# Gate row of a modulation in 1024-wide sums, and two sets of rounded projection weights in place of three

## The chip, the cores and the metric

The kernel runs on one core of a Trainium2 chip. The metric is the device time of one execution in microseconds (us). The kernel before was timed in three runs: median 555.95 us, from 555.89 to 556.93. Its profile is of one further execution, which took 556.66 us, of which the profiled span is 554.9 us.

The engines are named as in the profile: PE is TensorE (matmul), PEld its weight load, DVE is VectorE, ACT is ScalarE, POOL is GpSimd, SP is SyncE, whose queue issues all DMAs here. An engine executes its instructions in the order of its own list. A line number such as L542 is a line of the kernel before.

## What is computed

One decoder layer for 1024 tokens of width 1024, in fp32, cut to what matters here:

```
(shift, scale, gate) = silu(c) @ w_mod + b_mod        # w_mod: 1024 x 3072
h    = rmsnorm(x) * g_pre * (1 + scale) + shift
proj = h @ w_in                                       # the columns go to three head groups
y    = concat(mLSTM, sliding-window attention, stick-breaking attention)   # each gated by silu(z)
x    = x + gate * rmsnorm(y @ w_out) * g_post
```

The gate is one row of 1024 numbers: for column j the sum over the 1024 inputs d of silu(c)[d] * w_mod[d, 2048 + j], plus a bias.

## The kernel before

**Precision.** A weight matrix is used as two rounded parts: the hi part is a cast on ACT (L300), the lo part is the difference on POOL (L302, in two halves of 512 columns). A projection is three products: hi by hi, lo by hi, hi by lo.

**Projection items.** PE works through a list of items. Two are token-major (`mif`, `av`, class ProjT, L385). Sixteen are column blocks of `w_in` (class ProjD, L359), each with 48 matmuls of 128x512: 24 for the first 512 tokens, 24 for the second. The order at the start is mif, ak (block d7), av, then aq0, aq1, aq2 (d4, d5, d6), then the blocks of the stick-breaking heads and of the gates z. From aq1 on, the items are cut into pieces of a few matmuls, which stand between the matmuls of the head groups (`fill(n)`).

**Weights of an item.** `prep_load` issues the DMA of a block (512 KB) into a staging tile `w_d`, of which there are two. `prep_split` makes `wh_d` and `wl_d`; of these there are `nw` sets, three in this kernel. A set can be written again when PE has done the item that used it. Both steps have a raised priority.

**Order.** PE's order is written out by hand. That of DVE, ACT, POOL and SP is by hand up to the first projection; from there on a scheduler lays them out by readiness and priority.

**Start of the stretch.** While PE runs `mif`, DVE makes a causal convolution of three blocks of 128x1024: three products (L506) and nine sums (L509), in the order tap 1 of the blocks 0, 1, 2, then tap 2, then tap 3. Each finished block goes through a sigmoid on ACT (`cusg`, L513, two buffers) and a product on POOL (`cu`, L514). ACT's copies that empty the PSUM banks of `mif` (L446, L447) stand behind these sigmoids in ACT's list. PE's projections alternate between two banks.

**Gate row.** While PE runs `av`, the gate row is summed on DVE (`gate_row`, L534 to L542): column block by column block of 256, each in 8 products of 128x256 with one number of silu(c) per partition, added up in `gacc`. So there are 4 TENSOR_SCALAR and 28 SCALAR_TENSOR_TENSOR. The weights come in eight DMAs of 512 KB (`wg`, four buffers). On PE, behind the last matmul of `av`, `gate_sum` adds up the 128 partitions by a product with ones (`gbps`, L551), once for each half of 512 columns; DVE adds the bias (L552) and POOL multiplies (L553). Then aq0 runs through.

**What follows.** Behind aq0 the mLSTM chunks start. Of chunk c, `qps` (L674) and `kps` (L684) come first, then `sps` (L693), `cps` (L699) and `nps` (L715). `nps` needs `am` (L695 on DVE), the product of `sps` with a decay matrix `e`. That matrix comes from DVE (L664, when the DMA `mbc` has landed), then POOL's mask (L665), then ACT's exponential (L667).

Of the kernel before, what the change touches and what calls it, by code (L numbers as in the profile page):

```python
# [10 lines left out]
F32 = mybir.dt.float32  # L11
F32R = mybir.dt.float32r
AF = mybir.ActivationFunctionType
ALU = mybir.AluOpType
# [3 lines left out]
P = 128  # L18
D = 1024
S = 1024  # L20
KT = 8
# [25 lines left out]
def trunk(ctx: ExitStack, tc, x, w_ss, w_gate, rows, cols, w_mu, w_mif, w_dm, w_av, wqk, bif, alibi, w_out,  # L47
          out):
    nc = tc.nc
    V, A, G, T = nc.vector, nc.scalar, nc.gpsimd, nc.tensor  # L50

    def pool(name, bufs=1, side="left", space=None, stack=ctx):
        kw = dict(name=name, bufs=bufs, reuse_waits="tile")
        if space is not None:
            kw["space"] = space
        else:
            kw["side"] = side
        return stack.enter_context(tc.tile_pool(**kw))

    def f32(ap):  # L60
        return ap.bitcast(F32) if ap.dtype == F32R else ap

    def load(dst, src):
        nc.sync.dma_start(f32(dst), f32(src))
# [26 lines left out]
    csil = cp.tile([P, KT], F32, name="csil")  # L91
# [189 lines left out]
    tw = pool("tw", side="right", stack=tw_stk)  # L281
# [3 lines left out]

    def prep_load(key, src, shape, tok=False):
        n = int(np.prod(shape))
        p, w, nw = (tw, "t", 4) if tok else (fw, "w", 3)
        size = 2 * MIF if tok else D
        z = p.tile([P, size], F32, tag=w + "32", bufs=2, name=f"w_{key}")  # L290
        with tc.high_priority(offset=0 if tok else WPRI):
            load(z[:, 0:n], src)
        wready[key] = (z, n, shape, p, w, nw, size)
# [11 lines left out]
    def prep(key, src, shape, tok=False):  # L305
        prep_load(key, src, shape, tok)
        prep_split(key, tok)
# [26 lines left out]
    fw = pool("fw", stack=fw_stk)  # L334
    stg = pool("stg", stack=fw_stk)

    class ProjD:
# [5 lines left out]
        def prep(self, stage):  # L343
            if self.halves[0] == 0:
                if stage == 0:
                    prep_load(f"d{self.ti}", w_dm[self.ti], (KT, P))
                else:
                    prep_split(f"d{self.ti}")
# [156 lines left out]
    for j in range(3):  # L505
        V.tensor_scalar(out=cu[:, j, :], in0=mup[:, j, 0:S], scalar1=col[:, C_CW + 4 * j:C_CW + 4 * j + 1],  # L506
                        scalar2=col[:, C_CB + j:C_CB + j + 1], op0=ALU.mult, op1=ALU.add)
        for tap in range(1, 4):
            V.scalar_tensor_tensor(out=cu[:, j, :], in0=mup[:, j, tap:tap + S],  # L509
                                   scalar=col[:, C_CW + 4 * j + tap:C_CW + 4 * j + tap + 1], in1=cu[:, j, :],  # L510
                                   op0=ALU.mult, op1=ALU.add)
# [16 lines left out]
    def gate_row():  # L528
        gacc = gp_.tile([P, D], F32, name="gacc")
        rowb = gp_.tile([P, 2, D], F32, name="rowb")  # L530
        load(rowb, rows.partition_broadcast(P))
        for s_ in range(4):
            a = gacc[:, s_ * 256:(s_ + 1) * 256]
            for q in range(2):  # L534
                w = gw.tile([P, 4, 256], F32, tag="wg", bufs=4, name=f"wg{s_}_{q}")
                load(w, w_gate[s_][:, 4 * q:4 * q + 4, :])
                for i in range(4):
                    c = csil[:, 4 * q + i:4 * q + i + 1]
                    if q + i == 0:
                        V.tensor_scalar(out=a, in0=w[:, 0, :], scalar1=c, scalar2=None, op0=ALU.mult)  # L540
                    else:
                        V.scalar_tensor_tensor(out=a, in0=w[:, i, :], scalar=c, in1=a, op0=ALU.mult, op1=ALU.add)  # L542
        return gacc, rowb

    def gate_sum():
# [45 lines left out]
    for h in range(MH):  # L591
        V.tensor_tensor_scan(out=mp[:, 4 + h:36:4], data0=ga[:, h:32:4], data1=ga[:, 32 + h:64:4], initial=0.0,
                             op0=ALU.max, op1=ALU.add)
# [30 lines left out]
    gw_stk = ExitStack()  # L624
    gw = pool("gw", stack=gw_stk)
    gacc, rowb = gate_row()
    fill(GF[3])
    fill.through(I_AQ)
# [520 lines left out]
def lay_out(inputs):  # L1149
    f = {k: np.asarray(v) for k, v in inputs.items()}  # L1150
    w_mod = f["w_mod"][0]
    wm = w_mod.reshape(KT, P, 3, D)
    w_ss = wm[:, :, 0:2, :].reshape(KT, P, 2, KT, P).transpose(3, 1, 0, 2, 4).reshape(KT, P, KT, 2 * P)
    w_gate = wm[:, :, 2, :].reshape(KT, P, 4, 256).transpose(2, 1, 0, 3)
    b_mod = f["b_mod"][0].reshape(3, D)
    colT = lambda v: v.reshape(-1, P).T
    cw = f["m_conv_w"][0].reshape(4, 3, P).transpose(2, 1, 0).reshape(P, 12)
    cols = np.concatenate([colT(b_mod[0]), colT(b_mod[1]), colT(f["g_pre"][0]), colT(f["c"][0]), cw,
                           colT(f["m_conv_b"][0]), colT(f["m_norm_g"][0]), colT(f["m_skip"][0]),
                           np.broadcast_to(f["a_sinks"][0], (P, AH))], axis=1)  # L1160
    rows = np.stack([b_mod[2], f["g_post"][0]])
    w = f["w_in"][0]
    w_mu = w[:, 0:384].reshape(KT, P, 384)
    tok = lambda m: m.reshape(4, 2, P, m.shape[1]).transpose(0, 2, 1, 3).reshape(4, P, 2 * m.shape[1])
    w_mif = tok(w[:, 384:776])
    w_av = tok(np.concatenate([w[:, 1672:1800], w[:, 2696:2952]], axis=1))
    dm = [w[:, o + j * P:o + (j + 1) * P].reshape(KT, P, P).transpose(1, 0, 2).reshape(P, D)
          for o, n in ((2184, 2), (2440, 2), (1160, 3), (1544, 1), (776, 3), (1800, 3), (2952, 2)) for j in range(n)]
    wqk = np.stack([f["m_wq"][0].transpose(2, 0, 1), f["m_wk"][0].transpose(2, 0, 1)], axis=1)
    bif = np.stack([np.tile(f["m_b_i"][0], NT), np.tile(f["m_b_f"][0], NT)], axis=1)  # L1170
    slopes = (2.0 ** (-8.0 * np.arange(1, AH + 1) / AH)).astype(np.float32)
    rel = P + np.arange(P)[:, None] - np.arange(2 * P)[None, :]
    ok = (rel >= 0) & (rel < P)
    alibi = np.where(ok[None], -slopes[:, None, None] * rel.astype(np.float32), np.float32(NEG))
    return dict(x=f["x"][0], w_ss=w_ss, w_gate=w_gate, rows=rows, cols=cols, w_mu=w_mu, w_mif=w_mif,
                w_dm=np.stack(dm), w_av=w_av, wqk=wqk, bif=bif, alibi=alibi.astype(np.float32).transpose(1, 0, 2),
                w_out=f["w_out"][0].reshape(KT, P, D))
# [17 lines left out]
```

## Time and profile before

| | us |
|---|---|
| median of three runs | 555.95 |
| the profiled execution | 556.66 |
| its span | 554.9 |
| PE busy | 527.5 (95%) |
| DVE busy | 336.3 (61%) |
| ACT busy | 250.5 (45%) |
| POOL busy | 222.4 (40%) |
| DMA, mean rate over the span | 174 GB/s |

The busy share of PE counts its time at either clock level: the table of 40 slices shows a granted clock below full speed in two places besides the first and last slices, at about 83 to 97 us and 152 to 166 us. The chain that ended last runs over PE for 80% of the span, over DVE for 10%, over ACT for 5%. A wait of another engine counts for the end only where PE waits for it in turn.

### The profile page before, as it was taken

The page shows a single profiled execution, that of the slowest core. Times are in us where ns is not written, and L with a number is a line of the kernel's source. Part 1 is how long each engine was busy: PE and PEld are TensorE (multiplying, and loading weights), DVE is VectorE, ACT ScalarE, POOL GpSimd, SP SyncE. Part 2 cuts the span into 40 slices and gives each one's busy share as a digit, 9 for nine tenths or more (in the row PEclk, how much of TensorE's full clock was granted, in tenths as well). Part 3 has the DMA queues.
Part 4 walks back from the last instruction along what each step waited for, and adds up shares of the span by engine and source line. Part 5 has one row for each costly group of instructions (what it writes and reads, how often), then busy time and mean ns, then how long its engine had stood idle before and what let it go on. Part 6 is the DMA issues. An engine that isn't in the chain of part 4 may idle for free.

```text
span 554.9 us, 8574 instructions
## 1 busy us (share of the span) xinstructions
PE 527.5 (95%) x2953; PEld 452.3 (82%) x2953; DVE 336.3 (61%) x774; ACT 250.5 (45%) x571; POOL 222.4 (40%) x206
## 2 busy tenths in 40 slices
PE   4799997999979999999999999999999999999995
PEld 3577897989958998877788788888888888788884
DVE  5686692053835778669797669787887443108232
ACT  5643442351103333336877668676767332114100
POOL 2355796340014253324343456683765333111000
PEclk9999997999989999999999999999999999999998
DMA  8981451127976455399964269555211159606421
GB/s 298 418 310 57 139 206 59 57 98 188 322 219 210 149 172 153 104 265 259 251 205 138 92 186 281 170 129 194 96 59 76 39 171 403 245 16 236 144 80 71
DMA packets 63659, 96.57 MB, mean 174 GB/s; under 512 B 17600, under 2 KB 36992, under 8 KB 63488
## 3 DMA queue, kind: packets, MB, share of 16 engines
q1 hardware_dynamic: 63616, 96.03, 54.5%
q8 instruction: 23, 0.38, 0.3%
q14 instruction: 20, 0.16, 0.1%
HBM read 69.24 MB, written 25.20 MB: 170 GB/s over the span
## 4 chain that ended last, share of the span: by engine, by line
PE 80%; DVE 10%; ACT 5%; issue 2%; POOL 1%; DMA 1%; DVEq 0%; POOLq 0%; SPq 0%; ACTq 0%
PE pd L359 26%; PE ptav L385 6%; PE mu L233 6%; PE op L1112 5%; PE op L1111 5%; PE op L1110 5%; PE ptmif L385 3%; PE tp L997 3%; DVE cu L509 3%; ACT zb L850 3%; PE ops L1016 2%; PE ops L1015 2%; DVE zb L860 2%; PE z L966 2%; PE xps L166 2%
## 5 line engine op out<-in xcount | busy, mean ns | idle before, releaser
L359 PE MATMUL pd<-hh,wh_d 128*128 128x512 f32 x256 | 72.2, 407 | 0.0
L359 PE MATMUL pd<-hh,wl_d 128*128 128x512 f32 x256 | 71.2, 400 | 0.0
L359 PE MATMUL pd<-hl,wh_d 128*128 128x512 f32 x256 | 70.6, 398 | 0.0
L359 PEld LDWEIGHTS pd<-hh,wh_d 128*128 128x128 f32 x256 | 47.1, 192 | 8.9 <-issue 0.6
L359 PEld LDWEIGHTS pd<-hl,wh_d 128*128 128x128 f32 x256 | 46.1, 188 | 8.1
L359 PEld LDWEIGHTS pd<-hh,wl_d 128*128 128x128 f32 x256 | 45.9, 189 | 7.8
L302 POOL TENSOR_TENSOR wl_d<-w_d,wh_d 128x512 fp32r<-128x512 f32 x32 | 46.5, 1475 | 13.5 <-ACT wh_d L300 13.5
L1112 PE MATMUL op<-wol,hh 128*128 128x512 f32 x128 | 50.7, 396 | 0.0
L1110 PE MATMUL op<-woh,hh 128*128 128x512 f32 x128 | 50.6, 396 | 0.0
L1111 PE MATMUL op<-woh,hl 128*128 128x512 f32 x128 | 50.6, 396 | 0.0
L71 DVE TENSOR_TENSOR al<-tp,ah 128x512 fp32r<-128x512 f32 (+2 forms) x56 | 27.4, 494 | 19.9 <-ACT ah L70 19.6
L985 POOL TENSOR_TENSOR sg<-sg,pr 128x512 f32<-128x512 f32 (+1 forms) x30 | 31.1, 1041 | 19.7 <-DVE pr L983 19.4
L860 POOL TENSOR_SCALAR zb<-zb,mx 128x256 f32<-128x256 f32 (+1 forms) x24 | 21.6, 911 | 41.9 <-ACT ph L70 17.0
L70 ACT CAST ah<-tp 128x512 fp32r<-128x512 f32 (+2 forms) x56 | 24.4, 437 | 28.7 <-PE tp L997 21.5
L1123 ACT ACTIVATE sj<-op 128x512 f32<-128x512 f32 x16 | 9.5, 597 | 50.2 <-PE op L1112 47.7
L1112 PEld LDWEIGHTS op<-wol,hh 128*128 128x128 f32 x128 | 24.0, 188 | 6.0 <-POOL wol L71 0.2
L1111 PEld LDWEIGHTS op<-woh,hl 128*128 128x128 f32 x128 | 24.0, 188 | 5.9
L1110 PEld LDWEIGHTS op<-woh,hh 128*128 128x128 f32 x128 | 24.0, 188 | 5.8
L1127 POOL TENSOR_TENSOR st<-st,mhalf 128x1 f32<-128x1 f32 x8 | 4.4, 555 | 57.2 <-DVE st L1126 57.2
L850 ACT ACTIVATE zb<-zb,mx 128x256 f32<-128x256 f32 (+1 forms) x48 | 23.2, 485 | 8.3 <-DVE mx L840 6.7
L983 DVE TENSOR_TENSOR_SCAN pr<-z,mzero 128x128 f32<-128x128 f32 (+3 forms) x32 | 25.5, 813 | 1.0 <-ACT z L974 0.7
L385 PE MATMUL ptmif<-wh_mif,hh 128*128 128x392 f32 x64 | 23.2, 362 | 3.0 <-ACT igf L447 3.0
(247 smaller groups left out, 1338.7 us busy)
## 6 DMA issues: line engine op xcount, KB each, us to landing
wm<-in_w_ss_dram SPq DMA_DIRECT2D x16, 512.0 KB, 7.9
w_d<-in_w_dm_dram SPq DMA_DIRECT2D x16, 512.0 KB, 3.8
xt<-in_x_dram SPq DMA_DIRECT2D x8, 512.0 KB, 8.3
wg<-in_w_gate_dram SPq DMA_DIRECT2D x8, 512.0 KB, 6.3
wo<-in_w_out_dram SPq DMA_DIRECT2D x8, 512.0 KB, 5.4
xr<-in_x_dram SPq DMA_DIRECT2D x8, 512.0 KB, 4.4
out_dram<-ot SPq DMA_DIRECT2D x16, 256.0 KB, 2.4
hh<-d_yh SPq DMA_DIRECT2D x12, 256.0 KB, 5.8
```

What stands on the lines that cost most here:

```text
L71: e_lo.tensor_tensor(out=dst_l, in0=src, in1=dst_h.bitcast(F32), op=ALU.subtract)
L233: T.matmul(mu_acc[j][n], w[:, cs], h[:, k, t], start=(k == 0 and w is wh and h is hh), stop=(k == KT - 1 and h is hl))
L302: G.tensor_tensor(out=wl[:, a:b], in0=z[:, a:b], in1=wh.bitcast(F32)[:, a:b], op=ALU.subtract)
L359: T.matmul(ps, w[:, k, :], h[:, k, t], start=(k == 0 and w is wh and h is hh), stop=(k == KT - 1 and h is hl))
L385: T.matmul(ps[:, 0:self.N], h[:, k, t], w[:, k % 2, :], start=(k == 0 and q == 0), stop=(k == KT - 1 and q == 2))
L850: A.activation(z, z, AF.Exp, bias=nm[:, h:h + 1], accum_out=sm[:, h:h + 1])
L860: (G if h >= 6 - NPOOL else V).tensor_scalar(out=z, in0=z, scalar1=sm[:, h:h + 1], scalar2=None, op0=ALU.mult)
L983: V.tensor_tensor_scan(out=rev(pr), data0=rev(zps), data1=mzero[:, 0:1].to_broadcast([P, w]), initial=1.0 if nxt is None else nxt, op0=ALU ...
L985: (G if w > 256 and (h > 0 or i > 3) else V).tensor_tensor(out=sg[:, 0:w], in0=sg[:, 0:w], in1=pr[:, 1:w + 1], op=ALU.mult)
L1110: T.matmul(o, hh[:, k, t], woh[:, k, cs], start=(k == 0), stop=False)
L1111: T.matmul(o, hl[:, k, t], woh[:, k, cs], start=False, stop=False)
L1112: T.matmul(o, hh[:, k, t], wol[:, k, cs], start=False, stop=(k == KT - 1))
```

## The change

The gate weights are laid out by blocks of 128 inputs instead of blocks of 256 columns, and the gate row is summed in eight instructions of 128x1024 (one TENSOR_SCALAR, seven SCALAR_TENSOR_TENSOR). The DMAs are still eight of 512 KB, with 4 KB per partition in one piece. The sets of `wh_d` and `wl_d` are two instead of three.

```diff
     def prep_load(key, src, shape, tok=False):
         n = int(np.prod(shape))
-        p, w, nw = (tw, "t", 4) if tok else (fw, "w", 3)
+        p, w, nw = (tw, "t", 4) if tok else (fw, "w", 2)
...
-        for s_ in range(4):
-            a = gacc[:, s_ * 256:(s_ + 1) * 256]
-            for q in range(2):
-                w = gw.tile([P, 4, 256], F32, tag="wg", bufs=4, name=f"wg{s_}_{q}")
-                load(w, w_gate[s_][:, 4 * q:4 * q + 4, :])
-                for i in range(4):
-                    c = csil[:, 4 * q + i:4 * q + i + 1]
-                    if q + i == 0:
-                        V.tensor_scalar(out=a, in0=w[:, 0, :], scalar1=c, scalar2=None, op0=ALU.mult)
-                    else:
-                        V.scalar_tensor_tensor(out=a, in0=w[:, i, :], scalar=c, in1=a, op0=ALU.mult, op1=ALU.add)
+        for k in range(KT):
+            w = gw.tile([P, D], F32, tag="wg", bufs=4, name=f"wg{k}")
+            load(w, w_gate[k])
+            c = csil[:, k:k + 1]
+            if k == 0:
+                V.tensor_scalar(out=gacc, in0=w, scalar1=c, scalar2=None, op0=ALU.mult)
+            else:
+                V.scalar_tensor_tensor(out=gacc, in0=w, scalar=c, in1=gacc, op0=ALU.mult, op1=ALU.add)
...
-    w_gate = wm[:, :, 2, :].reshape(KT, P, 4, 256).transpose(2, 1, 0, 3)
+    w_gate = wm[:, :, 2, :]
```

The scheduler lays out the lists of DVE, ACT, POOL and SP anew; PE's list stays as it is, but for line numbers. Lines from L543 on have a number lower by three in the changed kernel.

DVE, from the third last piece of `av` to the end of the gate row (`vsl5` to `vsl7` empty the banks of `av`; `wg3_1` is the second half of the inputs of the last column block). Before:

```order
L71 TENSOR_TENSOR vsl6_1497<-ptav_6_1471,vsh6_1496 128x384
L542 SCALAR_TENSOR_TENSOR gacc_1328<-wg2_1_1361,csil_73,gacc_1328 128x256 x2
L540 TENSOR_SCALAR gacc_1328<-wg3_0_1367,csil_73 128x256
L542 SCALAR_TENSOR_TENSOR gacc_1328<-wg3_0_1367,csil_73,gacc_1328 128x256 x3
L542 SCALAR_TENSOR_TENSOR gacc_1328<-wg3_1_1373,csil_73,gacc_1328 128x256
L552 TENSOR_TENSOR gbc_74<-gbps0_1534,rowb_1329 128x512
L542 SCALAR_TENSOR_TENSOR gacc_1328<-wg3_1_1373,csil_73,gacc_1328 128x256
L71 TENSOR_TENSOR vsl7_1528<-ptav_7_1502,vsh7_1527 128x384
L542 SCALAR_TENSOR_TENSOR gacc_1328<-wg3_1_1373,csil_73,gacc_1328 128x256 x2
L552 TENSOR_TENSOR gbc_74<-gbps1_1538,rowb_1329 128x512
```

The same place in the changed kernel:

```order
L71 TENSOR_TENSOR vsl5_1442<-ptav_5_1416,vsh5_1441 128x384
L539 SCALAR_TENSOR_TENSOR gacc_1328<-wg5_1346,csil_73,gacc_1328 128x1024
L539 SCALAR_TENSOR_TENSOR gacc_1328<-wg6_1349,csil_73,gacc_1328 128x1024
L71 TENSOR_TENSOR vsl6_1473<-ptav_6_1447,vsh6_1472 128x384
L539 SCALAR_TENSOR_TENSOR gacc_1328<-wg7_1352,csil_73,gacc_1328 128x1024
L71 TENSOR_TENSOR vsl7_1504<-ptav_7_1478,vsh7_1503 128x384
L549 TENSOR_TENSOR gbc_74<-gbps0_1510,rowb_1329 128x512
L549 TENSOR_TENSOR gbc_74<-gbps1_1514,rowb_1329 128x512
```

Before, the bias addition of the first half (L552, it waits for PE) stands ahead of the last three sums and of `vsl7`. Now all sums stand ahead of `vsl7` and of both bias additions.

POOL, from the last weights of `av` to the second chunk of the mLSTM (`d7`, `d4`, `d5`, `d6`, `d0` are the blocks of ak, aq0, aq1, aq2 and the first stick-breaking item; `e0`, `e1` the decay matrices of the chunks 0 and 1; the rows of L746 prepare the output of a chunk). Before:

```order
L302 TENSOR_TENSOR wl_d6_1713<-w_d6_1664,wh_d6_1712 128x512 x2
L553 TENSOR_TENSOR gbc_74<-gbc_74,rowb_1329 128x512 x2
L665 AFFINE_SELECT e0_1566<-e0_1566 128x512
L665 AFFINE_SELECT e1_1658<-e1_1658 128x512
L746 TENSOR_TENSOR cu_799<-cu_799,col_62 128x3x128
L302 TENSOR_TENSOR wl_d0_2040<-w_d0_1967,wh_d0_2039 128x512 x2
L746 TENSOR_TENSOR cu_799<-cu_799,col_62 128x3x128
```

The same place in the changed kernel:

```order
L302 TENSOR_TENSOR wl_d5_1563<-w_d5_1548,wh_d5_1562 128x512 x2
L550 TENSOR_TENSOR gbc_74<-gbc_74,rowb_1329 128x512 x2
L302 TENSOR_TENSOR wl_d6_1689<-w_d6_1640,wh_d6_1688 128x512 x2
L743 TENSOR_TENSOR cu_799<-cu_799,col_62 128x3x128
L662 AFFINE_SELECT e0_1542<-e0_1542 128x512
L662 AFFINE_SELECT e1_1634<-e1_1634 128x512
L743 TENSOR_TENSOR cu_799<-cu_799,col_62 128x3x128
```

Further up in POOL's list the split of d5, third behind d7 and d4 and ahead of the three products L514, has gone; every block is now split one item later. Here the split of the next block and the product of L746 have moved ahead of the masks of `e0` and `e1`.

ACT at the same place (`sh_aq0_1` empties the bank of the second half of aq0). Before:

```order
L421 ACTIVATE sh_aq0_0_1604<-pd4_0_1574 128x512
L667 ACTIVATE e0_1566<-e0_1566 128x512
L667 ACTIVATE e1_1658<-e1_1658 128x512
L421 ACTIVATE sh_aq0_1_1635<-pd4_1_1610 128x512
L300 CAST wh_d0_2039<-w_d0_1967 128x1024
L677 COPY q1_0_1646<-qps0_1641 96x512
```

The same place in the changed kernel:

```order
L421 ACTIVATE sh_aq0_0_1580<-pd4_0_1550 128x512
L300 CAST wh_d6_1688<-w_d6_1640 128x1024
L421 ACTIVATE sh_aq0_1_1611<-pd4_1_1586 128x512
L674 COPY q1_0_1622<-qps0_1617 96x512
L664 ACTIVATE e0_1542<-e0_1542 128x512
L664 ACTIVATE e1_1634<-e1_1634 128x512
```

The cast has moved ahead of the evacuation of the same item's second half, here and at the ends of nearly all later items, and the exponentials of `e0` and `e1` behind the copy of `q`.

## Rows read from the trace of the kernel before

**Rows 1.** PE's waits over the span: total us, times, longest us.
```profile
PE gbps L551 <- DVE gacc L542: 3.2, 1, 3.2
PE ptmif L385 <- ACT igf L447: 3.0, 1, 3.0
```
**Rows 2.** Windows: us; PE, PEld, DVE, ACT, POOL busy (count); PEclk; DMA share; GB/s.
```profile
90.80:94.00 3.20, 3.14 (x10) 3.14 (x11) 0.09 (x1) 0.46 (x3) 3.13 (x2) 0.50 0.00 0
...
260.00:270.00 10.00, 9.10 (x54) 7.83 (x53) 8.31 (x32) 7.36 (x24) 3.32 (x4) 1.00 1.08 257
```
**Rows 3.** Timeline of PE around the first wait: start us, us, instruction [idle before].
```profile
87.54 0.33 PE L385 MATMUL ptmif<-wl_mif,hh 128*128 128x392 f32 x1
90.86 0.70 PE L385 MATMUL ptmif<-wh_mif,hh 128*128 128x392 f32 x1 [2.98 <-ACT igf L447]
...
96.90 0.34 PE L385 MATMUL ptmif<-wh_mif,hh 128*128 128x392 f32 x1
```
**Rows 4.** Timeline of ACT, the third sigmoid of the convolution.
```profile
89.32 1.06 ACT L513 ACTIVATE cusg<-cu 128x1024 f32<-128x1024 f32 x1 [2.36 <-POOL cu L514]
```
**Rows 5.** Timeline of POOL, splits beside the convolution.
```profile
70.62 12.96 POOL L302 TENSOR_TENSOR wl_d<-w_d,wh_d 128x512 fp32r<-128x512 f32 x6 [3.40 <-ACT wh_d L300]
```
**Rows 6.** Timeline of DVE: all nine sums of the convolution, then its last two.
```profile
69.98 17.08 DVE L509 SCALAR_TENSOR_TENSOR cu<-mup,col,cu 128x1024 f32<-128x1024 f32 x9
...
84.59 2.47 DVE L509 SCALAR_TENSOR_TENSOR cu<-mup,col,cu 128x1024 f32<-128x1024 f32 x2
```
**Rows 7.** Timeline of PE, from the gate row to the first chunk.
```profile
153.31 1.02 PE L551 MATMUL gbps<-gacc,ones 128*128 128x512 f32 x2
157.52 1.26 PE L551 MATMUL gbps<-gacc,ones 128*128 128x512 f32 x2 [3.19 <-DVE gacc L542]
158.05 3.99 PE L359 MATMUL pd<-hh,wh_d 128*128 128x512 f32 x8
161.87 2.00 PE L359 MATMUL pd<-hh,wl_d 128*128 128x512 f32 x8
...
170.96 1.04 PE L674 MATMUL qps<-cuh,gm 96*96 96x128 f32 x8
...
176.15 1.03 PE L715 MATMUL nps<-v,am 128*128 128x97 f32 x8
```
**Rows 8.** Timeline of DVE in the gate row.
```profile
134.42 1.53 DVE L542 SCALAR_TENSOR_TENSOR gacc<-wg,csil,gacc 128x256 f32<-128x256 f32 x3
...
140.11 1.53 DVE L542 SCALAR_TENSOR_TENSOR gacc<-wg,csil,gacc 128x256 f32<-128x256 f32 x3 [2.34 <-DMA wg<-in_w_gate_dram]
...
154.36 0.69 DVE L552 TENSOR_TENSOR gbc<-gbps,rowb 128x512 f32<-128x512 f32 x1 [0.73 <-PE gbps L551]
...
155.83 1.54 DVE L542 SCALAR_TENSOR_TENSOR gacc<-wg,csil,gacc 128x256 f32<-128x256 f32 x2
```
**Rows 9.** The tile wg: SP's issue ns (min/median/max), first and last start; landing.
```profile
L64 SPq DMA_DIRECT2D wg<-in_w_gate_dram x8: 384/746/1863, 129.5 to 146.3; - x8
...
DMA to landing us min/median/max: 4.5/6.3/7.0
```
**Rows 10.** The chain of waits, the shortest stretch of a whole item.
```profile
448.10 10.89 PE pd L359 x48
```
**Rows 11.** Timeline of POOL at the first chunk.
```profile
167.77 1.56 POOL L665 TENSOR_SCALAR_AFFINE_SELECT e<-e 128x512 f32<-128x512 f32 x2 [6.92 <-DVE e L664]
172.41 0.83 POOL L746 TENSOR_TENSOR cu<-cu,col 128x384 f32<-128x384 f32 x1 [3.08 <-PE kps L684]
173.20 2.50 POOL L302 TENSOR_TENSOR wl_d<-w_d,wh_d 128x512 fp32r<-128x512 f32 x2
```
**Rows 12.** Timeline of ACT at the first chunk.
```profile
168.78 1.22 ACT L667 ACTIVATE e<-e 128x512 f32<-128x512 f32 x2 [2.46 <-POOL e L665]
...
171.70 1.04 ACT L300 CAST wh_d<-w_d 128x1024 fp32r<-128x1024 f32 x1
```
**Rows 13.** Timeline of DVE at the first chunk.
```profile
166.96 1.28 DVE L664 TENSOR_TENSOR e<-tcol,mbc 128x512 f32<-128x512 f32 x2
```

## The prediction

> **What bounds the kernel now.** I read the table of PE's waits first. PE works almost throughout, so the end moves by what PE waits, and by the clock at which it runs. Behind the start, the two longest waits are one of 3.2 us for the gate row's sum, and one of 3.0 us for ACT's copy of the gate pre-activations [rows 1]. The change touches both places.
>
> Next I looked at what each wait leaves behind. Where the first one ends, PE is granted 0.50 of its clock, which is the lower of its two levels, 1.2 GHz [rows 2]. The timeline shows the price: from the start at 90.86 to the start at 96.90 there are 18 steps in 6.04 us [rows 3]. A step of 512 columns takes 10.89 / 48 = 0.227 us at full clock [rows 10], so 392 columns should take 0.174 (an estimate by the columns), and 18 steps 3.1 us. The low clock costs 2.9 us, about as much as the wait itself. The second wait does the same: eight matmuls take 3.99 us behind it and eight later ones 2.00 [rows 7].
>
> Then I followed each wait back. The first: the copy stands in ACT's list behind the third sigmoid, which waits for a buffer that POOL's first product frees at 89.3 [rows 4]; that product waits for the first block's sigmoid, and this one for the seventh sum on DVE, which ends where the eighth starts, at 84.59 [rows 6]. The second: the gate row's last sums run at 155.8, though PE ended `av` at 153.3, because in DVE's list a bias addition that waits for PE's first product stands ahead of them and runs at 154.36 [rows 7, 8].
>
> **First place: one split less beside the convolution.** Sums beside POOL's splits take long: the first seven need 84.59 - 69.98 = 14.6 us, the last two, alone, 2.47 together, so 1.24 each [rows 6]. The first of the seven ran mostly alone, which leaves (14.6 - 1.2) / 6 = 2.23 for each of the six beside POOL's six halves, which took 12.96 / 6 = 2.16 each [rows 5]. The two engines work in turns: 2.23 is 1.24 of DVE and 1.0 of POOL. Without the split of d5 POOL does four halves, and the sixth and seventh sum run alone: 2 x 0.99 = 2.0 us. All behind it comes 2.0 earlier: the first sigmoid, POOL's product, the third sigmoid, the copy, PE. (At 83.7 the ninth sum and POOL's first product now want to start together. Whichever goes first, the third sigmoid needs the end of both, so the chain is as long.) The next matmul could have started at 87.54 + 0.17 = 87.71. It starts at 90.86, and will at 88.9: 1.2 us stay.
>
> Does 1.2 us still lower the clock? A stretch with 0.9 us of idle time ran at full clock [rows 2]. That is the nearest row, so I take no fall and a gain of 2.0 + 2.9 = 4.9 us. With the fall it is 2.0.
>
> **Second place: the gate row.** Now 28 sums at 1.53 / 3 = 0.51 us and four products become eight instructions of 1024 columns. The same operation and width alone took 1.24, beside POOL 2.23, and four narrow ones take 2.04 [rows 6, 8]; I take 1.24, since POOL has no splits to do there. The first load stays where it is; the second landed at 140.1 [rows 8]. From there: sums 1 and 2 to 142.6, `vsl4`, sums 3 and 4 to 145.6. A buffer is free at its first use now, not after four sums, so the last load's issue, 146.3 before [rows 9], follows the third sum at about 144.5. With the median of 6.3 us it lands at 150.8 and with the longest of 7.0 at 151.5 [rows 9]; the last sum ends at 152.1 to 152.8, ahead of 153.3. No bias addition stands in front of it any more.
>
> So PE goes on at 153.3. The two products need 2 x 1.02 us at most, aq0 starts at 155.3 and takes 10.9, and the first chunk begins at 166.2 in place of 170.96 [rows 7, 10]. The gain is 4.8 us: the wait, the low clock behind it, less the second product.
>
> **A new wait at the first chunk.** The cast of d6 can only start when PE has done aq0; the time of that is T below (170.96 before). In ACT's list it stands ahead of the evacuation, in POOL's list its split and the product of L746 stand ahead of the masks of `e0` and `e1`. Before, the masks ran at 167.77, ahead of T, and d6's set had long been made. Now: cast from T + 0.2, 1.04; two halves 2.50; L746 0.83; mask 1.56 / 2 = 0.78; exponential 1.22 / 2 = 0.61; then `am`, of the size of L664, 1.28 / 2 = 0.64 [rows 11 to 13]. The sum is T + 6.6. PE came to `nps` at 176.15, T + 5.2 [rows 7]. PE waits 1.4 us. Behind the waiting cast on ACT stand the evacuation and the copy of `q`, which need the same end of aq0; behind `am` on DVE stand only later steps of the chunks.
>
> DVE's two L664 now fall beside the split, since `mbc` stands behind aq0's stores in SP's list and lands later against T. If they and the halves take turns as the sums of the convolution did, 2 x 0.64 come on top, and the wait is 2.7. I take 2.0, between the ends, with both kept for the range.
>
> The Trainium skill ("SBUF — State Buffer", section "Who interferes with whom") says that a VectorE instruction with two SBUF inputs and a GpSimd instruction that reads SBUF exclude each other for a whole instruction, whoever came first. The convolution agrees, 2.23 against 1.24. By that rule the wait is 2.7 us and the total 0.7 us worse than below; without it 0.6 better.
>
> **What costs nothing.** With two sets, an item's weights are split while the item before it runs: 1.04 + 2.50 us, against 10.9 for the shortest item [rows 10 to 12]. Cover that is gone would cost up to 3.5 an item. ACT's evacuations at item ends come 1.04 later, behind the cast; the bank is written again 24 matmuls later, 5.4 us. The staging load of the next block is issued an item ahead as before.
>
> **Sum.** 4.9 + 4.8 - 2.0 = 7.7 us, against the profiled execution's 556.66: 549.0. The runs' median lies 0.7 below that execution, so 548.3 for the median.
>
> **Rivals.**
> 1. The clock falls in spite of the shorter first wait. For it: 3.0 us of idle time ended at 0.50. Against it: the stretch with 0.9 us. Price 2.9: 551.2. Chance 0.12.
> 2. The gate row is not earlier, because a wide sum costs what four narrow ones do (2.04), or because the loads bunch up. From 140.1 seven sums and three `vsl` of about 0.55 end at 156.0, and PE waits as before. Without the 4.8: 553.1. For it: 2.23 a sum beside POOL. Against it: 1.24 alone. Chance 0.10.
> 3. The new wait is at its upper end and lowers the clock: 0.7 + 2.9 more, 551.9. Chance 0.08.
> 4. The new wait does not come, as the masks need not wait so long, and the first place closes fully: 2.0 + 1.2 better, 545.1. Chance 0.05.
> 5. Slower: ACT's cast ahead of the evacuation. At 14 item ends it delays an evacuation by 1.04. Where ACT and DVE feed PE closely, in the attention stretch at 240 to 350, each can reach PE. Exposed at all 14 it is 14.6 us: 562.9. It decides from eight ends on (8 x 1.04 against 7.7). Against it: the cast before stood directly behind the evacuation, and ACT's work is the same. Chance 0.05, of which 0.02 is for so many ends that nothing is left to measure.
>
> **How the numbers follow.** The forecast has the other 0.60. Its own range is 546 to 551, from the terms 4.9 and 4.8 with half a us each and the wait of 1.4 to 2.7. The range of 544.5 to 552 takes in rivals 1, 3 and 4, the lowest with half a us to spare, and leaves out 2 and 5. Below 0.2%, 1.1 us, a measurement of this kernel can't tell a difference. Faster is everything but rival 5: 0.95; same 0.02, slower 0.03.
>
> **What would show it.** PE's wait for `igf` falls from 3.0 to about 1 us, with full clock behind it; POOL's splits beside the convolution are four. The wait for `gacc` is gone, the wide sums last 1.2 to 1.3 us, and eight matmuls behind `gbps` take 2.0. A new wait of `nps` for `am` of 1.4 to 2.7 us appears, with the mask behind the split. From there on the two timelines run in parallel, some 8 us apart. I am wrong if the gap closes after the first chunk, if a wide sum lasts 2 us, or if half clock shows behind either place.

## The result, and the profile after

The changed kernel took 553.0 us (median of four runs, 552.9 to 553.6), against 556.3 for the kernel before (four runs, three of them those of the table above). The ratio is 0.9944, 95% interval 0.9932 to 0.9957: 3.3 us faster, less than half of the 7.7 forecast, and outside the range. The profiled execution took 553.0 us with a span of 551.2.

PE's waits of the changed kernel (total us, times, longest):

```profile
PE ao L880 <- DVE ya L893: 2.5, 4, 1.1
PE ops L1012 <- DVE ys L1019: 1.8, 2, 1.5
...
PE cps L696 <- DVE ku L683: 1.5, 1, 1.5
...
PE nps L712 <- DVE am L692: 1.0, 1, 1.0
...
PE ptmif L385 <- ACT igf L447: 0.9, 1, 0.9
```

The wait for `gacc` of [rows 1] is gone and that for `igf` is 0.9 in place of 3.0. Three waits have grown or come in: for `ku` and `am` in the first chunk, for `ys` and `ya` in the attention stretch.

PE's list is the same in both kernels, so the start of each matmul can be compared with the start of the same matmul before. That shows where the time went:

| matmul | before | after | difference | what lies between |
|---|---|---|---|---|
| last one ahead of the wait for `igf` | 87.54 | 87.91 | +0.37 | the start |
| 18 steps behind it | 96.90 | 92.51 | -4.39 | first place: -4.76 |
| first `qps` | 170.96 | 161.54 | -9.42 | gate row: -5.02 |
| an `nps` of a later chunk | 200.02 | 193.59 | -6.43 | first chunk: +2.99 |
| an `sps` of a later chunk | 230.06 | 223.60 | -6.46 | -0.03 |
| a `z`, stick-breaking | 352.00 | 348.54 | -3.46 | attention stretch: +3.00 |
| the last | 548.23 | 544.56 | -3.67 | -0.20 |

Both gains came as forecast. The first chunk took back 3.0 and not 2.0, and 3.0 more went in a stretch where I expected nothing.

The first place, in the timelines of the changed kernel. PE:

```profile
87.91 0.33 PE L385 MATMUL ptmif<-wl_mif,hh 128*128 128x392 f32 x1
89.18 0.45 PE L385 MATMUL ptmif<-wh_mif,hh 128*128 128x392 f32 x1 [0.93 <-ACT igf L447]
...
92.51 0.35 PE L385 MATMUL ptmif<-wh_mif,hh 128*128 128x392 f32 x1
```

and the window of the 18 steps (columns as in [rows 2]):

```profile
89.18:92.50 3.32, 3.32 (x18) 3.32 (x19) 0.09 (x1) 0.39 (x2) 3.10 (x2) 1.00 0.00 0
```

The gap between the first two starts is 1.27 us in place of 3.32, and the 18 steps that took 6.04 at 0.50 [rows 2, 3] take 3.33 at 1.00. DVE's nine sums take 15.00 us in place of 17.08 [rows 6], since POOL splits two blocks beside them, not three:

```profile
71.02 8.46 POOL L302 TENSOR_TENSOR wl_d<-w_d,wh_d 128x512 fp32r<-128x512 f32 x4 [3.41 <-ACT wh_d L300]
```

The gate row on DVE in the changed kernel, in rows that answer to [rows 8]:

```profile
135.21 2.61 DVE L539 SCALAR_TENSOR_TENSOR gacc<-wg,csil,gacc 128x1024 f32<-128x1024 f32 x2 [1.82 <-DMA wg<-in_w_gate_dram]
...
146.28 1.28 DVE L539 SCALAR_TENSOR_TENSOR gacc<-wg,csil,gacc 128x1024 f32<-128x1024 f32 x1 [0.17 <-DMA wg<-in_w_gate_dram]
```

A wide sum takes 1.28 (1.24 was taken), the last ends at 147.6, and PE, 4.4 us earlier than before, starts the product at 148.9 without a wait.

### The profile page after: what moved, and what is told of

Its sections match the earlier page's. It is cut to its first block, busy times and chain, and to the rows that moved or that the text cites. A ratio compares the mean times of both kernels' runs of the same rounds, so it can differ in the third digit from the quotient of the medians.

```text
span 551.2 us, 8550 instructions
## 1 busy us (share of the span) xinstructions
PE 523.9 (95%) x2953; PEld 449.0 (81%) x2953; DVE 332.5 (60%) x750; ACT 250.3 (45%) x571; POOL 220.6 (40%) x206
## 4 chain that ended last, share of the span: by engine, by line
PE 78%; DVE 10%; DMA 4%; ACT 3%; issue 2%; POOL 2%; SPq 1%; DVEq 0%; POOLq 0%; ACTq 0%
PE pd L359 24%; PE ptav L385 6%; PE mu L233 6%; PE op L1109 5%; PE op L1108 5%; PE op L1107 5%; PE tp L994 3%; DMA ka<-d_akl 3%; PE ptmif L385 2%; DVE cu L509 2%; PE ops L1012 2%; PE ops L1013 2%; PE xps L166 2%; PE z L963 2%; PE mr L197 1%
## 5 line engine op out<-in xcount | busy, mean ns | idle before, releaser
L359 PE MATMUL pd<-hh,wh_d 128*128 128x512 f32 x256 | 70.6, 400 | 0.0
L302 POOL TENSOR_TENSOR wl_d<-w_d,wh_d 128x512 fp32r<-128x512 f32 x32 | 44.0, 1398 | 29.1 <-ACT wh_d L300 19.6
L982 POOL TENSOR_TENSOR sg<-sg,pr 128x512 f32<-128x512 f32 (+1 forms) x30 | 31.1, 1041 | 20.8 <-DVE pr L980 20.6
L71 DVE TENSOR_TENSOR al<-tp,ah 128x512 fp32r<-128x512 f32 (+2 forms) x56 | 27.4, 493 | 16.7 <-ACT ah L70 16.0
L969 ACT ACTIVATE sg<-z 128x512 f32<-128x512 f32 (+3 forms) x48 | 23.8, 496 | 1.3 <-PE z L966 1.1
```

What stands on the lines that cost most here:

```text
L71: e_lo.tensor_tensor(out=dst_l, in0=src, in1=dst_h.bitcast(F32), op=ALU.subtract)
L302: G.tensor_tensor(out=wl[:, a:b], in0=z[:, a:b], in1=wh.bitcast(F32)[:, a:b], op=ALU.subtract)
L359: T.matmul(ps, w[:, k, :], h[:, k, t], start=(k == 0 and w is wh and h is hh), stop=(k == KT - 1 and h is hl))
L969: A.activation(sg[:, 0:w], zps[:, 0:w], AF.Sigmoid)
L982: (G if w > 256 and (h > 0 or i > 3) else V).tensor_tensor(out=sg[:, 0:w], in0=sg[:, 0:w], in1=pr[:, 1:w + 1], op=ALU.mult)
```

## The first chunk: what PE waits for

PE's timeline there, answering to [rows 7]:

```profile
161.54 1.04 PE L671 MATMUL qps<-cuh,gm 96*96 96x128 f32 x8
...
166.50 0.92 PE L696 MATMUL cps<-v,ku 128*96 128x97 f32 x8 [1.53 <-DVE ku L683]
...
169.59 1.13 PE L712 MATMUL nps<-v,am 128*128 128x97 f32 x8 [1.00 <-DVE am L692]
```

and DVE's, answering to [rows 13]:

```profile
164.97 1.00 DVE L661 TENSOR_TENSOR e<-tcol,mbc 128x512 f32<-128x512 f32 x1 [7.35 <-DMA mbc<-d_m]
165.90 0.54 DVE L683 TENSOR_TENSOR ku<-kps,tcol 128x384 f32<-128x384 f32 x1
```

The larger wait is one that I had not foreseen. On DVE, `ku` (`kps` times a weight, which `cps` needs) stands behind `e0`, and `e0` waits for the DMA `mbc`. The chain of waits gives that DMA's start and the time that the chain spends in it:

```profile
159.93 0.54 SPq L64
160.47 0.04 issue
160.51 3.65 DMA mbc<-d_m
```

It was issued at 160.5, 1.0 us ahead of the first `qps`. Before, PE came there at 170.96, 7.8 us behind the issue of `mbc`, so late that `e0` and `e1` ran at 166.96 [rows 7, 13]. The issue on SP, before and after:

```profile
163.12 1.08 SPq L64 DMA_DIRECT2D mbc<-d_m  x2
```

```profile
160.51 0.94 SPq L64 DMA_DIRECT2D mbc<-d_m  x2
```

So `mbc` is issued 2.6 us earlier and PE comes 9.4 us earlier. In the changed kernel SP issues one DMA after another without a pause from 149 to 164 us, about 0.7 us each, and `mbc` is the 17th, now behind the first stores of aq0. PE now overtakes it.

**Theory.** The 3.0 us belong to the gate row's being earlier, against an SP queue that does not gain as much. The 3.0 us of the attention stretch belong to the two sets: POOL's splits stand earlier in its list and fall beside short DVE instructions. **Rival A**: whatever runs early runs into DMAs there too. **Rival B**: two sets are too few and weights come late. **Rival C**: not the split but the evacuation behind ACT's cast comes late.

## Each half of the change alone

The wide sums alone, with `nw` at 3:

```diff
-        p, w, nw = (tw, "t", 4) if tok else (fw, "w", 2)
+        p, w, nw = (tw, "t", 4) if tok else (fw, "w", 3)
```

> The gate row in 1024-wide sums alone, three sets as before. Theory (the changed kernel's gain is eaten between 230 and 351 us because with two sets POOL's splits come earlier and fall beside short DVE instructions): the gate row gives its 5.0 us and nothing is lost in the attention stretch; the first chunk may cost 0 to 1.5 us, since its decay inputs come late here too. Time 551 to 552.8 (before 556.0 to 556.3). Rival A (whatever runs some us earlier runs into DMAs that do not come earlier): 2 us or so are lost again after 230 us, time 553 to 554.5. First place as before: PE waits 3.0 us for igf, half clock behind it.

Measured: 554.2 us, ratio 0.9959 (0.9945 to 0.9974). By the same matmuls as in the table: gate row -5.01, first chunk +3.35, attention stretch -0.10. (The first place shows -1.30, though nothing was changed there; the last section comes back to it.) So rival A is out, and the first chunk's loss comes with three sets as well. The median lies 1.4 above what I expected, as the loss there is larger than my 0 to 1.5. DVE at the first chunk in this kernel:

```profile
169.26 0.69 DVE L661 TENSOR_TENSOR e<-tcol,mbc 128x512 f32<-128x512 f32 x1 [7.42 <-DMA mbc<-d_m]
```

It waits for `mbc` again, which was issued at 164.81; the first `qps` was at 165.76. The mask of `e0` stands ahead of POOL's split here (170.03 and 170.64), and the loss is there all the same.

Two sets alone, with the gate row in 256-wide sums as before (the change's first hunk only):

> Two sets alone, gate row in 256-wide sums as before. Theory: the first place gives 4.8 us, the attention stretch takes 2 to 3 us and the first chunk 0 to 2 back, so the time is 552.5 to 555.5. Rival A (lost only where all runs early by more than the first place's gain): the stretch loses under 1 us, time 551 to 552. Rival B (PE waits for weights of the items, one set too few): PE's waits name wh_d or wl_d.

Measured: 555.0 us, ratio 0.9983 (0.9971 to 0.9994). First place -4.78, first chunk -0.06, attention stretch +2.57. `e0` and `e1` ran at 162.6, since `mbc` is issued 7.9 us ahead of the first `qps` again (158.75 and 166.60), and their masks stand ahead of d6's split. So the order on which I had based the new wait does not come with two sets alone. PE's waits name no weights (rival B), but the same two as the changed kernel's:

```profile
PE ao L883 <- DVE ya L896: 2.5, 4, 1.1
PE ops L1015 <- DVE ys L1022: 1.8, 2, 1.5
```

The losses of the halves, 3.35 and 2.57, lie close to the two of the whole, 2.99 and 3.00.

## The attention stretch: the split and the cast

The largest single loss is at `ops`, the stick-breaking heads' product with v, which waits for `ys` on DVE. In the changed kernel POOL has, at that place:

```profile
340.76 2.59 POOL L302 TENSOR_TENSOR wl_d<-w_d,wh_d 128x512 fp32r<-128x512 f32 x2 [0.25 <-ACT wh_d L300]
344.52 1.30 POOL L484 TENSOR_TENSOR d_ym_91r<-d_ym_91r,gs_mz 128x512 f32<-128x512 f32 x1 [1.17 <-DVE d_ym_91r L473]
```

and DVE:

```profile
341.02 2.61 DVE L982 TENSOR_TENSOR sg<-sg,pr 128x128 f32<-128x128 f32 x2
...
346.93 0.66 DVE L1019 TENSOR_TENSOR ys<-ops,otmp 64x512 f32<-64x512 f32 x1
```

Two products L982, of 128 and of 256 columns, take 2.61 us, as long as the two halves of the split beside them. Before, the same two stood alone:

```profile
346.22 0.27 DVE L985 TENSOR_TENSOR sg<-sg,pr 128x128 f32<-128x128 f32 x1
...
347.00 0.42 DVE L985 TENSOR_TENSOR sg<-sg,pr 128x256 f32<-128x256 f32 x1
```

and the split came at 348.5, behind L484, in POOL's timeline:

```profile
347.17 1.41 POOL L484 TENSOR_TENSOR d_ym_91r<-d_ym_91r,gs_mz 128x512 f32<-128x512 f32 x1 [1.46 <-DVE d_ym_91r L473]
348.54 2.54 POOL L302 TENSOR_TENSOR wl_d<-w_d,wh_d 128x512 fp32r<-128x512 f32 x2
```

The Trainium skill ("SBUF — State Buffer", section "Who interferes with whom") says that the second of the two to issue is blocked until the first is done. These rows agree: the two products end at 342.20 and 343.63, 0.15 and 0.28 us behind the ends of the two halves beside them.

To undo the order alone, cast and split get a lower priority:

```diff
     def prep_split(key, tok=False):
...
-        with tc.high_priority(offset=0 if tok else WPRI):
+        with tc.high_priority(offset=0 if tok else 100):
```

> The changed kernel with the cast and the split at priority 100 in place of 400: in ACT's list the evacuation of an item's second half stands ahead of the cast again, in POOL's list the product L484 ahead of the split, and at the first chunk the mask of e0 ahead of d6's split. Theory: 2 to 2.8 us of the attention stretch come back, and about 1 us at the first chunk (no more PE wait for am): 549.3 to 551 (changed kernel 553.0). Rival A or B (early running, or one set too few): no change, 552.5 to 553.5.

Measured: 550.7 us, ratio 0.9905 (0.9889 to 0.9921). The attention stretch loses 1.10 in place of 3.00; the two products take 0.27 and 0.41 again and PE's wait for `ys` falls from 1.8 to 0.4. At the first chunk I was wrong: the wait for `am` goes as expected, but the one for `ku` grows to 2.3, and the loss there stays at 2.71.

This moves the cast and the split together. To part them, the next kernel leaves ACT's cast where the change puts it, and takes POOL's reads away:

```diff
+    NOLO = ('d0', 'd1', 'd2', 'd3', 'd8', 'd9', 'd10', 'd11', 'd12', 'd13')
...
             for a, b in ((0, n // 2), (n // 2, n)):
-                G.tensor_tensor(out=wl[:, a:b], in0=z[:, a:b], in1=wh.bitcast(F32)[:, a:b], op=ALU.subtract)
+                (G.memset(wl.bitcast(F32)[:, a:b], 0.0), G.tensor_tensor(out=wl[:, a:a + 8], ...)) if key in NOLO else G.tensor_tensor(...)
```

> The changed kernel, in which POOL's split of the ten blocks d0 to d3 and d8 to d13 writes zeros (MEMSET) and takes the difference only for 8 of each 512 columns, so the lo part of these weights is left out; ACT's list stays nearly as in the changed kernel, the cast ahead of the evacuation. Theory, if it is POOL's reads of SBUF that stretch DVE: the short DVE instructions (L835, L836, L982) keep their length, and 2 to 2.8 us come back: 550.2 to 551. Rival C (it is the evacuation behind ACT's cast that is late, not the split): no change, 552.5 to 553.5.

Measured: 550.0 us, ratio 0.9888 (0.9873 to 0.9903). The stretch now gains 0.43, so in sum all 3.00 are gone, and rival C is out: the casts stood ahead of the evacuations still. (POOL is also busy for less time: the zeros take 0.53 a half and run ahead of the cast, the differences 0.20. That it is not POOL's own lateness shows in the lengths of DVE's instructions.) Two rows of DVE where PE waits for `ya` at 267 us, first in the changed kernel:

```profile
264.94 0.49 DVE L835 TENSOR_TENSOR mx<-mx,col 128x6 f32<-128x6 f32 x1
...
265.82 0.86 DVE L836 TENSOR_SCALAR mx<-mx 128x6 f32<-128x6 f32 x1
```

then without the split's reads:

```profile
264.54 0.14 DVE L835 TENSOR_TENSOR mx<-mx,col 128x6 f32<-128x6 f32 x1
...
265.17 0.16 DVE L836 TENSOR_SCALAR mx<-mx 128x6 f32<-128x6 f32 x1
```

and, for comparison, in the kernel before:

```profile
272.34 0.54 DVE L838 TENSOR_TENSOR mx<-mx,col 128x6 f32<-128x6 f32 x1
...
273.27 0.15 DVE L839 TENSOR_SCALAR mx<-mx 128x6 f32<-128x6 f32 x1
```

Six columns took 0.86 us. The first of the two was stretched before as well; the second was not, as the split started 1.2 us ahead of DVE's `ya` there (270.29 and 271.54) and starts with it now (264.13 and 264.14). In POOL's list it has moved back here, behind two more products `zb`. By the same section of the Trainium skill the product of two SBUF inputs contends, and `tensor_scalar` can too, with its one input, in a mode that takes both ports; the two rows agree with it, though no row shows the mode.

PE's wait at 295 us goes back to the split at 283.4. This one stands where it stood, 0.93 us ahead of `ya` in both kernels, but DVE's list has changed beside it: L835 now stands ahead of two others and meets the second half (284.67 to 285.96) from its start. In the changed kernel, then in the kernel before:

```profile
284.67 1.32 DVE L835 TENSOR_TENSOR mx<-mx,col 128x6 f32<-128x6 f32 x1
```

```profile
292.08 0.64 DVE L838 TENSOR_TENSOR mx<-mx,col 128x6 f32<-128x6 f32 x1
```

Last, the same for the one block whose split is at 340.8 (`NOLO = ('d11',)`):

> The changed kernel, in which the split of the one block d11 writes zeros and takes the difference only for 8 of each 512 columns (the lo part of that block is left out). Theory (this split, at 340.8 us, doubles the products L982 on DVE beside it and PE waits for ys): L982 beside it takes 0.3 and 0.45 us again, PE's wait for ys there falls from 1.9 to 0.3 us, nothing else changes, so 1.6 us less: 551.2 to 551.6. Rival (the cast of d11 ahead of the evacuation): the wait stays, 552.8 to 553.3.

Measured: 551.0 us, ratio 0.9905 (0.9886 to 0.9923); the attention stretch +0.99 in place of +3.00, and 1.63 of the difference at that one `ops`. The two products on DVE:

```profile
340.73 0.65 DVE L982 TENSOR_TENSOR sg<-sg,pr 128x128 f32<-128x128 f32 x2
```

The wait went as expected; the time is 0.2 below the range, as 0.4 more came back elsewhere in the stretch. One collision of 2.6 us, with two instructions that take 0.7, was half of the loss.

## The first chunk: the queue

In the next kernel `mbc` is issued first; of the lists of DVE, ACT and POOL only the part at the first chunk moves:

```diff
-        load(mbc, d_m[c4, :].partition_broadcast(P))
+        with tc.high_priority(offset=100): load(mbc, d_m[c4, :].partition_broadcast(P))
```

> The changed kernel with the loads of mbc at a raised priority, so that SP issues them ahead of the cuh loads and of aq0's stores. Only the lists at the first chunk move: the masks of e0 and e1 stand ahead of d6's split on POOL, e0 and e1 ahead of ku on DVE, e0's exponential ahead of the cast on ACT. Theory (the first chunk waits because SP's queue issues mbc late against an aq0 that now starts early): the 3.0 us that PE loses there come back, 2 to 3 of them to the end: 550 to 551 (changed kernel 553.0), and nothing changes in the attention stretch, where 2.8 are still lost. Rival (it is the cast and the split, not mbc): PE still waits 1 us or more for am or ku, 552 to 553.

Measured: 551.25 us, ratio 0.9912 (0.9894 to 0.9930), 0.25 above the range. The waits for `ku` and `am` are gone, but the first chunk still loses 1.46, by a wait that took their place. PE's timeline:

```profile
160.82 0.64 PE L671 MATMUL qps<-cuh,gm 96*96 96x128 f32 x4
162.46 0.65 PE L671 MATMUL qps<-cuh,gm 96*96 96x128 f32 x4 [1.00 <-DMA cuh<-cu]
```

What is moved ahead in a full queue pushes another back: now `cuh`, the chunk's inputs, comes late. In front of both SP issues `ka` and `va`, the keys and values of the first attention pair, which PE uses at 232 us. The next kernel holds these five loads back, by short copies into the tiles that depend on a late chunk:

```diff
-        va = p.tile([P, 3, 2, P], F32R, tag="va", bufs=1, name=f"va{i}")
+        va = p.tile([P, 3, 2, P], F32R, tag="va", bufs=1, name=f"va{i}"); (V.tensor_copy(ka[:, 0, :, 0:1], st[NT - 2]["e"][:, 0, 0:2].unsqueeze(2)), V.tensor_copy(va[:, 0, 0, 0:1], st[NT - 2]["e"][:, 0, 0:1])) if i == 0 else None
```

> The changed kernel with mbc issued first, and with the five loads of ka and va of the first attention pair held back: two short copies write into ka and va from the decay matrix of chunk 6, and the loads that overwrite them have to wait for that. Theory (at the first chunk the bound is the time that SP needs to issue what stands ahead of cuh and mbc): the wait of 1.2 us for cuh that came in place of the waits for ku and am goes, so 1.0 to 1.3 us less than with mbc first alone: 549.8 to 550.5 (mbc first alone 551.25). The copies on DVE cost less than 0.2 us. Rival (cuh is late for another reason, its own transfer or a buffer): the wait stays and so does the time, 551 to 551.6; or the attention stretch waits for ka, 552 and more.

Measured: 549.7 us, ratio 0.9894 (0.9868 to 0.9919); the first chunk loses nothing (-0.06). (The interval overlaps that of `mbc` first alone; the trace decides.) SP has `mbc` out at 151 and waits for its next work at 156:

```profile
151.18 1.38 SPq L64 DMA_DIRECT2D mbc<-d_m  x2
152.60 3.70 SPq L64 DMA_DIRECT2D cuh<-cu  x4
157.21 0.34 SPq L64 DMA_DIRECT2D d_aqh<-sh_aq  x1
```

The wide sums alone, with `mbc` first, say whose loss it was:

> The 1024-wide sums alone, three sets, with mbc issued first. Theory (the first chunk's loss belongs to the gate row's being earlier, not to the two sets): the 3.35 us that the wide sums alone lost at the first chunk come back: 550.3 to 551.5 (wide alone 554.2 in the median of a wide spread, its profile 552.7 in span). Rival: 553 to 554.

Measured: 552.4 us, ratio 0.9925 (0.9908 to 0.9942): 1.7 less than the wide sums alone and 0.9 above the range I gave. The first chunk loses 1.38 in place of 3.35; what is left is the wait for `cuh`, as with `mbc` first in the changed kernel. So the loss is the gate row's. In the runs with an early `mbc` the masks also stand ahead of d6's split again; what the order alone would cost beside an early `mbc` no run shows.

## Both repairs together

> The changed kernel with both: cast and split at priority 100 (evacuation ahead of the cast again), and mbc issued first. Theory: the two losses are separate places and the gains add: 2.2 (as the run with the cast behind showed) and 2.5 to 3.0 from the first chunk, 547.5 to 549. Rival (one hides the other): 550 to 551, as with one alone.

Measured: 549.75 us, ratio 0.9884 (0.9865 to 0.9902), 0.75 above the range: the first chunk loses 1.36, by `cuh` again. With `ka` and `va` held back as well:

> The changed kernel with all three: cast and split behind the evacuation (priority 100), mbc issued first, ka and va held back. Theory: 1.1 to 1.5 us less than the two without the last (549.75): 548.2 to 548.7, which is what the prediction had for the changed kernel. Rival (other losses come in their place): 549.5 and more.

Measured: 548.5 us, ratio 0.9882 (0.9855 to 0.9909). First place -4.75, gate row -5.01, first chunk -0.06, attention stretch +0.87. Its median lies 4.5 below the changed kernel's, near the 548.3 that I predicted for the change as it stood. By the ratio the last step can't be told from noise (0.9882 against 0.9884; one of the six runs took 551.2); what it did shows in the trace, where the first chunk loses nothing in place of 1.36. Its longest waits of PE behind the start:

```profile
PE ao L880 <- DVE ya L893: 1.7, 3, 0.9
...
PE yps L741 <- DVE hn L732: 1.3, 2, 0.7
```

By the trace, most of the 0.87 left in the stretch goes back to one more collision. PE's matmuls at 324.7 and 328.9 lose 0.61 and 0.36, behind a chain on DVE in which the first product L982 ran beside a split (318.36 to 320.95) and took 0.65 longer than before (0.41, at 327.59):

```profile
318.75 1.06 DVE L982 TENSOR_TENSOR sg<-sg,pr 128x128 f32<-128x128 f32 x1
```

No run tests it in the repaired kernel. In the run without the split's reads the first two products L982 took 0.88 and 1.52 there (319.79 and 321.30), beside two other products of POOL, L484 and L71, so it is not the splits alone that collide.

## Why the prediction was wrong

- **First place, 4.9: right.** 4.76. POOL's four halves, the wait of 0.9 and full clock behind it came as worked out. About 1.2 of the 2.9 for the clock was luck of the profile compared with: two runs with the same wait paid less (last section).
- **Gate row, 4.8: right.** 5.02. The sums took 1.28 and ended 1.3 ahead of PE (forecast 0.5 to 1.2).
- **The new wait at the first chunk, -2.0: wrong in mechanism and too small.** The step that failed is "cast from T + 0.2, 1.04; two halves 2.50; ...": it took the cast and the split for the bound. With the mask ahead of the split and `mbc` as late, the wait for `am` went, and the loss stayed at 2.71; with `mbc` and `cuh` in time it was -0.06. The bound was SP's queue: `mbc` late, and behind `e0` the `ku`, of which I had no term. I had seen that `mbc` "lands later against T", and used it only for a surcharge of 0.64 a piece. It cost 2.99.
- **"What costs nothing": wrong, and the largest error, 3.0.** I asked whether an evacuation 1.04 later reaches PE, and dismissed rival 5 because "ACT's work is the same". What I put at nothing there was that POOL's splits and DVE's instructions meet anew. At 340.8 the split moved ahead of L484, at 264 it moved behind two products `zb`, at 283 it stayed and L835 moved towards it; each time a DVE instruction that PE waits for was stretched. I had the rule and a price at the convolution, and did not take it to the other places. "From there on the two timelines run in parallel" failed at 267, 295 and 348 us (+0.65, +0.68, +1.64).
- **Sum.** 4.76 + 5.02 - 2.99 - 3.00 + 0.23 = 4.0, and 0.37 of the start off it: 3.7 in the profile, 3.3 in the medians. The range of 546 to 551 was also wider than its terms give (546.7 to 550.0), and the 553.0 lie outside it.

## What to carry to other kernels

When a buffer count changes, the scheduler moves every step that uses the buffer: list all places where the order of an engine's list has changed, on every engine that follows, and ask at each which instruction of another engine now runs beside it. Behind any gain, ask of the next stage whether its DMAs are issued by then; a queue that is busy without a pause does not come as much earlier as the engines (here 2.6 us against 9.4).

## What was not expected of the hardware

- The price of a collision is not set by the DVE instruction's own length. Beside halves of 1.27 to 1.34 us, six columns took 0.86 and 1.32 us in place of 0.15, and a product L982 up to 1.5. The eight of them at 322 to 342 us in the changed kernel (ns, min/median/max):

```profile
L982 DVE TENSOR_TENSOR sg<-sg,pr x8: 267/737/1511, 322.2 to 342.1; 128x128 f32<-128x128 f32 x3, 128x256 f32<-128x256 f32 x3, 128x384 f32<-128x384 f32 x1, 128x512 f32<-128x512 f32 x1
```

  My "turns" at the convolution, where 1.24 became 2.23, hid this, since both sides were about equally long there (1.24 and, a half alone, about 1.3).
- Behind the same wait of 3.0 us for `igf`, the wide sums alone took 4.77 us for the 18 steps that took 6.04 before [rows 3]. Windows of that kernel, columns as in [rows 2]:

```profile
91.90:95.10 3.20, 3.16 (x10) 3.16 (x11) 0.09 (x1) 0.44 (x2) 2.94 (x2) 0.50 0.00 0
95.10:97.00 1.90, 1.90 (x12) 1.90 (x11) 0.00 (x0) 0.00 (x0) 0.00 (x0) 0.98 0.52 154
```

  The wide sums with `mbc` first took 4.87, also behind a wait of 3.0. So the price of a fallen clock differs by over a microsecond between runs of like kernels. The 39 executions of the kernel before that were run beside the experiments point the same way: four had a mean granted clock of 0.995 or 0.996 and took 553.4 to 554.4 us, the others 0.987 to 0.993 and 555.1 to 558.1. So part of the gain at both places removes a loss that the kernel before does not have in every execution; which place the four were spared no trace shows.
